# Second feed-forward of a hybrid retention and attention block: weights prepared three steps ahead, turned features fetched by SyncE and used later

## The chip, the core and the metric

The kernel runs on one core of a Trainium2 chip. The metric is device microseconds of one execution, taken as the median of several runs.

## The reference, cut to what matters

One layer with three parts: a feed-forward, a mixer (retention beside sparse attention) and a second feed-forward, for 512 tokens and 16 meta tokens. The change is in the last part, for 512 tokens with D = 1024 and 2816 hidden features, all in fp32.

```python
def swiglu(u, w_gate, w_up, w_down):
    return (jax.nn.silu(u @ w_gate) * (u @ w_up)) @ w_down
...
        h = h + 0.5 * swiglu(rmsnorm(h, ffn1_norm[l]), ffn1_w_gate[l], ffn1_w_up[l], ffn1_w_down[l])
        h = h + hybrid_mixer(rmsnorm(h, mix_norm[l]), pos, k_top, w_in[l], w_ret_out[l], w_att_out[l], w_mix_out[l])
        h = h + 0.5 * swiglu(rmsnorm(h, ffn2_norm[l]), ffn2_w_gate[l], ffn2_w_up[l], ffn2_w_down[l])
    y = rmsnorm(h, final_norm)
```

## The kernel before

An fp32 product is made of three matmuls. Each factor is split in two: the upper part is a copy that ScalarE rounds (L323: `whi` of a weight, `hh` of the features), and the lower part is what VectorE gets by subtracting that copy (L324: `wlo`, `hl`). The products upper by upper, upper by lower and lower by upper are summed in PSUM.

The hidden features of the second feed-forward are done in six units of 512 columns (unit 4 has 256, the narrow one). Gate and up of a unit are 14 steps of twelve matmuls (class `Rows`, `steps`): seven products, each in two halves, of sums and differences of weight quarters and token quarters, so that seven products do the work of eight. `wsum` adds weight quarters on VectorE; `ws` is the buffer of the first sum, and w11, w12, w21 and w22 are the quarters, loaded by SyncE (SP). The results go to PSUM banks named X, Y, Z and V and from there to three rooms A, B and C in SBUF (`copy` on ScalarE, `add` on VectorE). `silu` runs on ScalarE, `gated` multiplies gate and up on VectorE. A and C then hold the gated features of half the tokens each.

The down-projection needs features on the partitions. `turn` does 32x32 transposes on VectorE into `cross`, writes them to DRAM in four stores (`hts`) and loads them back as `land`; stores and load are issued on GpSimd (POOL). `hidden(half)` splits a landed half into `hh` and `hl`. A down step (`down`, L2432) has 24 matmuls; unit i has four of them, woven into the gate and up steps of unit i+1, after steps 4, 7, 10 and 13 (`woven`). `take` adds four finished banks to the tokens on VectorE.

`steps_through` walks through all steps. It loads four steps ahead (`pre`), does the upper split of a step two steps ahead (`upper`) and its lower split in the middle of the present step (`lower`, then `catch_up`, which runs what stands in the list `late`). After a step's matmuls its entries of `posts_of` run: `put(3, ...)` is what follows step 3. On TensorE, ScalarE and VectorE the instructions stand in the order in which this code is written; on SP and POOL a scheduler orders the DMA issues. The weight parts have three buffers each. The down weights are loaded into two buffers `raw` of two halves each.

Of the kernel before, what the change touches and what calls it, by code (L numbers as in the profile page):

```python
# [11 lines left out]
F32 = mybir.dt.float32  # L12
# [69 lines left out]
def kernel(ctx: ExitStack, tc: tile.TileContext, x, meta, g1, wg1, wu1, wd1, gm,  # L82
# [245 lines left out]
    def steps_through(steps):  # L328


        ws = {}

        def pre(i):
            if i < len(steps):
                steps[i][0]()

        def upper(i):
            if i < len(steps):
                v = steps[i][1]()
                n, c = v.shape[1:]  # L340
                at = (*steps[i], w_at[0])[3]
                if len(steps[i]) > 4:
                    hi, lo = steps[i][4]()
                else:
                    hi, lo = (wpool.tile([P, 1024 + WPAD], F32R, tag=t, name=t, bufs=3)[:, at : at + n * c]
                              .rearrange("p (k c) -> p k c", k=n) for t in ("whi", "wlo"))
                ws[i] = (hi, lo, in_two(v, hi, lo))

        def lower(i):
            if i < len(steps):  # L350
                ws[i][2]()

        for i in range(4):
            pre(i)
        for i in range(2):
            upper(i)
            yield
            lower(i)
# [1558 lines left out]
    with pool("ao") as ao:  # L1917
# [219 lines left out]
        pipe = steps_through(steps)  # L2137
# [68 lines left out]
    class Rows:  # L2206
# [11 lines left out]
        FIRST = [("11", "B11", "X"), ("12", "B21", "Z"), ("12", "B22", "V"), ("11", "T2", "X"),  # L2218
                 ("s", "T1", "Y"), ("21", "T3", "X"), ("22", "T4", "X")]
# [29 lines left out]
        def bank(self, name):  # L2249
            tag = {"X": ("x", "d0")[self.first], "V": "d1"}.get(name, "z")  # L2250
            t = f2["ps"].tile([P, 1024], F32, tag=tag, name=f"psq{name}")
            self.d[name] = t.rearrange("p (t c) -> p t c", t=2)[:, :, : self.n]
# [21 lines left out]
        def turn(self, c, to, land, half):  # L2274

            src = self.room[c]
            n = 2 * self.n
            cross = f2["rooms"].tile([P, 1024], F32, tag=f"r{to}", name="cross")[:, :n].rearrange("p (b c t) -> p b c t", t=2, c=32)
# [6 lines left out]
            t = f2["rooms"].tile([P, 1024], F32, tag=f"r{land}", name="land")[:, :n].rearrange("p (k e) -> p k e", k=self.nf)  # L2285
            self.d["land", half] = t
            nc.gpsimd.dma_start(t, d.rearrange("(k p) a e -> p k (a e)", p=P))
# [15 lines left out]
        def steps(self, posts):  # L2303

            def step(i):
# [21 lines left out]
                return (lambda: None, lambda: self.q[n][:, j : j + 2], run)  # L2327
# [27 lines left out]
    def new_t(n):  # L2355
        t = f2["rooms"].tile([P, 1024], F32, tag="rD" if n == 2 else "rC", name=f"ts{n}") if n < 4 else None
# [19 lines left out]
    def fetch_tokens():  # L2376
# [10 lines left out]
        7: (lambda: u0.wsum(2, 0), lambda: u0.wsum(2, 2), fetch_tokens),  # L2387
# [47 lines left out]
    down_raw = []  # L2435
# [9 lines left out]
    def down(u, c, k0, banks, first=True, last=True, posts=(), taken_by=None, parts=None, b3=wide):  # L2445
# [3 lines left out]
        def pre():  # L2449
            if len(down_raw) % 2 == 0:  # L2450
                d["t"] = wpool.tile([P, 2048], F32, tag="raw", name="raw", bufs=2).rearrange("p (k c) -> p k c", k=4)
                down_raw.append(d["t"])
                d["raw"] = d["t"][:, :2]
            else:
                d["raw"] = down_raw[-1][:, 2:]
                down_raw.append(None)
            rows = slice((u.f0 + k0) * P, (u.f0 + k0 + 2) * P)
            nc.sync.dma_start(d["raw"], wd2[rows, c * S : (c + 1) * S].rearrange("(k p) c -> p k c", p=P))
# [59 lines left out]
    def posts_of(u):  # L2518
# [10 lines left out]
        if u.first:  # L2529
            put(0, lambda: u.wsum(4, 0))  # L2530
            put(1, lambda: u.copy("A", "p1", "X"), lambda: u.wsum(4, 2))
            put(2, lambda: new_t(2))
            put(3, lambda: split_t(2), lambda: u.add("A", "Z"))
            put(4, lambda: new_t(3))
            put(5, lambda: split_t(3), lambda: squares(0), lambda: squares(1))
            put(6, lambda: new_t(4), lambda: squares(2), lambda: squares(3), token_norm)
            put(7, lambda: u.copy("B", "u2", "X"), lambda: split_t(4), gate_of("A", 0))
            put(9, lambda: u.copy("C", "p5", "Y"), lambda: u.add("B", "Y"), lambda: u.add("B", "V"), gate_of("B", 1))
            put(11, lambda: u.add("C", "X"))
            loads = {6: "11", 8: "12", 9: "21", 11: "22"}  # L2540
        else:
            make = h4_tile if prev.nf == 2 else hid_tile
            a, b = (1, 3) if u.nf == 4 else (2, 4)
            put(0, lambda: u.wsum(2, 0))
# [10 lines left out]
            loads = {4: "11", 7: "21", 9: "12", 11: "22"}  # L2555
        put(12, lambda: u.gated("C", u.room["C"], u.room["B"], 1), lambda: u.turn("C", "D", "C", 1))
        put(13, lambda: u.gated("A", u.d["X"], u.room["A"], 0), lambda: late.append(lambda: u.turn("A", "B", "D", 0)))
# [3 lines left out]
        if u.first:  # L2561
            late_sums = [lambda: nxt.wsum(1, 0), lambda: nxt.wsum(1, 2)]
            put(13, lambda: late.extend(late_sums))
        return at

    def sums_of(u):
        return (lambda: u.wsum(1, 0), lambda: u.wsum(1, 2))
# [21 lines left out]
    n_units = len(steps)  # L2589
    u4, u5 = units[4:]  # L2590
    c0, c1 = [], []

    def kept_parts():
        t = places.tile([P, 4, S], F32R, tag="w11", name="kept")
        return t[:, 0:2], t[:, 2:4]
# [84 lines left out]
```

## Time and profile before

| | |
|---|---|
| median of 3 runs | 1566.19 us (1564.06 to 1566.45) |
| profiled execution | 1567.81 us, span 1566.0 us |
| mean granted TensorE clock | 0.981 |
| TensorE busy | 1504.8 us (96% of the span) |
| VectorE busy | 1139.6 us (73%) |
| ScalarE busy | 728.9 us (47%) |
| GpSimd busy | 169.9 us (11%) |

The span is the time from the first to the last instruction of the profiled execution. The second feed-forward is its last quarter: its first matmul is at 1149.5 us, its last at 1558. TensorE counts as busy while a matmul runs, also when it runs at the lower clock, so its share of the whole span tells little about one stretch of the program.

### The profile page before, as it was taken

The numbers are of one execution on the slowest core, as the hardware profiler recorded it, in microseconds if no ns is written. First come the engines' busy times: TensorE is split into PE (matmuls) and PEld (weight loads), VectorE is DVE, ScalarE is ACT, GpSimd is POOL, SyncE is SP. The second block draws the span as 40 slices with busy tenths as digits, with TensorE's granted clock in tenths as the row PEclk, the third lists the DMA queues.
The fourth block names the chain that finished last, engine by engine and source line by source line (L and its number), as shares of the span: only waits on it lengthen the run. The fifth ranks groups of instructions, "written<-read, shape, count | busy, mean of one in ns | idle before, by whom it ended". The sixth has DMA issues, their size and how long they took to land. (4 is left out here: it accounts for less than half of the span.)

```text
span 1566.0 us, 22512 instructions
## 1 busy us (share of the span) xinstructions
PE 1504.8 (96%) x8926; PEld 1328.5 (85%) x8926; DVE 1139.6 (73%) x1732; ACT 728.9 (47%) x1044; POOL 169.9 (11%) x250
## 2 busy tenths in 40 slices
PE   9999999999999999999999999999998798898997
PEld 8999999999888889898988889888876576677776
DVE  5997685776887766879787887774687585656765
ACT  5564362554454444433334476672354333433533
POOL 1000000002101020000000322310112010101110
PEclk9999999999999999999999999999999899999999
DMA  4233233247265171323233355664753242423431
GB/s 164 82 108 108 82 102 115 83 128 262 100 225 181 56 238 57 127 91 106 89 98 108 97 170 152 193 198 136 261 165 99 92 137 81 135 68 94 162 108 68
DMA packets 156698, 200.56 MB, mean 128 GB/s; under 512 B 13744, under 2 KB 111688, under 8 KB 155952
## 3 DMA queue, kind: packets, MB, share of 16 engines
q1 hardware_dynamic: 141232, 156.76, 31.0%
q0 software_dynamic: 11680, 35.51, 7.1%
q10 hardware_dynamic: 3680, 6.84, 1.2%
q8 instruction: 70, 1.15, 0.3%
q14 instruction: 36, 0.29, 0.1%
HBM read 168.91 MB, written 30.16 MB: 127 GB/s over the span
## 5 line engine op out<-in xcount | busy, mean ns | idle before, releaser
L324 DVE TENSOR_TENSOR wlo<-raw,whi 128x1024 fp32r<-128x1024 f32 (+2 forms) x155 | 172.5, 1116 | 49.2 <-ACT whi L323 49.1
L323 ACT ACTIVATE whi<-raw 128x1024 fp32r<-128x1024 f32 (+2 forms) x155 | 146.6, 949 | 104.0 <-PE psd L157 33.4
L324 DVE TENSOR_TENSOR wlo<-w,whi 128x1024 fp32r<-128x1024 f32 (+1 forms) x102 | 117.6, 1156 | 81.5 <-ACT whi L323 81.5
L323 ACT ACTIVATE whi<-w 128x1024 fp32r<-128x1024 f32 (+1 forms) x102 | 101.9, 1005 | 121.3 <-PE psd L2432 47.0
L2432 PE MATMUL psd<-whi,hh 128*128 128x512 f32 (+1 forms) x172 | 70.8, 412 | 15.9 <-ACT hh L323 12.2
L2432 PE MATMUL psd<-whi,hl 128*128 128x512 f32 (+1 forms) x172 | 70.8, 412 | 11.9 <-DVE hl L324 11.9
L157 PE MATMUL psro<-vo,whi 128*128 128x512 f32 x256 | 78.8, 389 | 0.0
L2432 PE MATMUL psd<-wlo,hh 128*128 128x512 f32 (+1 forms) x172 | 70.4, 409 | 1.7 <-DVE wlo L324 1.7
L157 PE MATMUL psd<-hl,whi 128*128 128x264 f32 x352 | 71.4, 284 | 0.0
L157 PE MATMUL psd<-hh,wlo 128*128 128x264 f32 x352 | 70.8, 283 | 0.0
L118 DVE TENSOR_TENSOR wlo<-raw,whi 128x1024 fp32r<-128x1024 f32 (+1 forms) x44 | 53.7, 1221 | 23.3 <-ACT whi L117 23.1
L157 PE MATMUL psd<-hh,whi 128*128 128x264 f32 x352 | 70.6, 282 | 0.0
L117 ACT ACTIVATE whi<-raw 128x1024 fp32r<-128x1024 f32 (+1 forms) x44 | 45.4, 1037 | 52.6 <-PE psat L157 17.3
L2319 PE MATMUL psqX<-whi,th 128*128 128x512 f32 (+1 forms) x144 | 56.0, 389 | 9.6 <-DVE p L2263 5.3
L2283 POOL DMA_DIRECT2D hts<-cross x48 | 30.7, 645 | 282.8 <-DVE cross L2280 282.7
L157 PE MATMUL psqX<-tl,whi 128*128 128x264 f32 x216 | 61.2, 283 | 0.0
L157 PE MATMUL psqX<-th,whi 128*128 128x264 f32 x216 | 61.1, 283 | 0.0
L157 PE MATMUL psqX<-th,wlo 128*128 128x264 f32 x216 | 61.1, 283 | 0.0
L2319 PE MATMUL psqX<-wlo,th 128*128 128x512 f32 (+1 forms) x144 | 55.7, 386 | 1.8 <-DVE wlo L324 1.8
L157 PEld LDWEIGHTS psro<-vo,whi 128*128 128x128 f32 x256 | 48.0, 188 | 10.1
L2432 PEld LDWEIGHTS psd<-whi,hh 128*128 128x128 f32 x172 | 35.1, 204 | 24.7 <-ACT hh L323 13.7
L2319 PE MATMUL psqX<-whi,tl 128*128 128x512 f32 (+1 forms) x144 | 55.1, 383 | 0.0
(547 smaller groups left out, 4704.1 us busy)
## 6 DMA issues: line engine op xcount, KB each, us to landing
raw<-in_w_in_dram SPq DMA_DIRECT2D x18, 1024.0 KB, 5.1
raw<-in_w_in_dram SPq DMA_DIRECT2D x33, 512.0 KB, 3.6
raw<-in_ffn_w_down_dram SPq DMA_DIRECT2D x24, 512.0 KB, 4.5
w<-in_w_in_dram SPq DMA_DIRECT2D x24, 512.0 KB, 6.2
raw<-in_ffn_w_up_dram SPq DMA_DIRECT2D x11, 1024.0 KB, 5.0
raw<-in_ffn_w_gate_dram SPq DMA_DIRECT2D x10, 1024.0 KB, 5.0
w<-in_ffn_w_up_dram SPq DMA_DIRECT2D x20, 512.0 KB, 4.7
w<-in_ffn_w_gate_dram SPq DMA_DIRECT2D x20, 512.0 KB, 4.5
```

The costliest lines, as they stand in the source:

```text
L117: nc.scalar.activation(hi, src, AF.Copy)
L118: eng.tensor_tensor(lo, src, hi.bitcast(F32), ALU.subtract)
L157: nc.tensor.matmul(o, a[:, k, :], b[:, sl], start=first and k == 0 and i == 0, stop=last and k == nk - 1 and i == 2, skip_group_check=onto)
L323: nc.scalar.activation(hi, src, AF.Copy)
L324: return lambda: nc.vector.tensor_tensor(lo, src, hi.bitcast(F32), ALU.subtract)
L2283: nc.gpsimd.dma_start(d.rearrange("(b i) a e -> a i b e", i=32)[a], cross[32 * a : 32 * a + 32].rearrange("p b c t -> p b (c t)"))
L2319: nc.tensor.matmul(ps[:, t], a, b[:, k, :], start=not onto and j + k + m == 0, stop=j + k == 3 and m == 2, skip_group_check=onto)
L2432: nc.tensor.matmul(ps, a, m[:, j, cs], start=first and i == 0, stop=last and i == 2)
```

## The change

Six edits, all in the second feed-forward.

1. From the first step of unit 0 to the last such step in the units, the upper split is done three steps ahead (`lead`). Three buffers don't do for that, so every fourth step puts its parts into a fourth pair, `wpair`, which lies in one of the two raw buffers. The down loads then have the two halves of the other one; a second raw buffer is used again by the last two down steps in the units (`last_raw`).
2. The `land` load is issued by SP (`fetch`), not by POOL.
3. The split of the turned features follows steps 2 and 4 in place of 1 and 3 (in the narrow unit 4 and 6 in place of 2 and 4), and the down steps follow steps 7, 9, 11 and 13 (in the narrow unit 8 and 13 in place of 6 and 13).
4. That split goes through its elements in another order: along the tokens, so that it writes next to the last element and reads every second one. Before it went along the pairs, reading next to the last and writing 128 elements further.
5. The first half of the second weight sum (`wsum(2, 0)`) is done with the sums ahead of the unit, not after step 0.
6. The first unit's products come in another order (`FIRST`): the product that used bank V now adds onto Y, which takes out one add on VectorE. The posts of that unit (weight sums, squares, token sums, copies) are placed anew, and the third and fourth token sums use the room of B, not of C. The quarters are loaded after other steps.

```diff
-    def steps_through(steps):
+    def steps_through(steps, lead=lambda i: 2):
...
-            upper(i + 2)
-            steps[i][2](ws.pop(i)[:2], lambda: lower(i + 2))
+            while at["upper"] <= min(i + lead(i), len(steps) - 1):
+                upper(at["upper"])
+                at["upper"] += 1
+            steps[i][2](ws.pop(i)[:2], lowers)
...
+        lead_from, lead_to = KD, []
+        pipe = steps_through(steps, lambda i: 3 if i >= lead_from and (not lead_to or i < lead_to[0]) else 2)
...
-        FIRST = [("11", "B11", "X"), ("12", "B21", "Z"), ("12", "B22", "V"), ("11", "T2", "X"),
-                 ("s", "T1", "Y"), ("21", "T3", "X"), ("22", "T4", "X")]
+        FIRST = [("11", "B11", "X"), ("12", "B21", "Z"), ("s", "T1", "Y"), ("11", "T2", "X"),
+                 ("12", "B22", "Y"), ("21", "T3", "X"), ("22", "T4", "X")]
...
+        def fetch(self, land, half):
+            d = hts[self.i % 2, half, : self.n]
+            t = f2["rooms"].tile([P, 1024], F32, tag=f"r{land}", name="land")[:, : 2 * self.n].rearrange("p (k e) -> p k e", k=self.nf)
             self.d["land", half] = t
-            nc.gpsimd.dma_start(t, d.rearrange("(k p) a e -> p k (a e)", p=P))
+            nc.sync.dma_start(t, d.rearrange("(k p) a e -> p k (a e)", p=P))
...
-                                                         ("p k (q t) -> p k q t", "p k (t q) -> p k q t", "p k (t q) -> p k q t"))]
+                                                         ("p k (q t) -> p k t q", "p k (t q) -> p k t q", "p k (t q) -> p k t q"))]
...
-            if len(down_raw) % 2 == 0:
-                d["t"] = wpool.tile([P, 2048], F32, tag="raw", name="raw", bufs=2).rearrange("p (k c) -> p k c", k=4)
...
+            held = last_raw if (u.i, c, k0) in ((4, 1, 0), (5, 0, 0)) else down_raw
+            if not held:
+                t = wpool.tile([P, 2048], F32, tag="raw", name="raw", bufs=2).rearrange("p (h k c) -> p h k c", h=2, k=2)
+                held.extend(t[:, i] for i in range(2))
+            held.append(held.pop(0))
+            d["raw"] = held[-1]
...
-            put(9, lambda: u.copy("C", "p5", "Y"), lambda: u.add("B", "Y"), lambda: u.add("B", "V"), gate_of("B", 1))
+            put(9, lambda: u.add("B", "Y"), gate_of("B", 1))
...
-            a, b = (1, 3) if u.nf == 4 else (2, 4)
-            put(0, lambda: u.wsum(2, 0))
+            a, b = (2, 4) if u.nf == 4 else (4, 6)
...
-            loads = {4: "11", 7: "21", 9: "12", 11: "22"}
+            loads = {6: "21", 7: "11", 9: "12", 11: "22"}
...
-        return (lambda: u.wsum(1, 0), lambda: u.wsum(1, 2))
+        return (lambda: u.wsum(1, 0), lambda: u.wsum(1, 2), lambda: u.wsum(2, 0))
...
-        woven(i, dict(zip((4, 7, 10, 13), d)))
+        woven(i, dict(zip((7, 9, 11, 13), d)))
...
-    woven(4, {6: d[0], 13: d[1]})
+    woven(4, {8: d[0], 13: d[1]})
...
+    for i in range(lead_from + 3, n_units - 2, 4):
+        steps[i] = (*steps[i], other_parts)
+        lead_to[:] = [i]
```

The first place is VectorE at the start of the third unit, behind the take of the second (a name ends in the number of its tile; `raw` is a down weight, `p1` the room of A). Before:

```order
L324 TENSOR_TENSOR wlo_12552<-w12_12358,whi_12551 128x1024
L2239 TENSOR_TENSOR w11_12186<-ws_12512,w11_12186 128x1024
L324 TENSOR_TENSOR wlo_12574<-w11_12186,whi_12573 128x1024
L324 TENSOR_TENSOR hl_12568<-land_12455,hh_12567 128x4x128x2
L324 TENSOR_TENSOR wlo_12592<-raw_12549,whi_12591 128x1024
L2263 TENSOR_TENSOR p1_12570<-psqZ_12576,p1_12570 128x1024
L324 TENSOR_TENSOR wlo_12612<-w11_12186,whi_12611 128x1024
L324 TENSOR_TENSOR hl_12568<-land_12498,hh_12567 128x4x128x2
```

In the changed kernel, from the same take on:

```order
L324 TENSOR_TENSOR wlo_12534<-w11_12237,whi_12533 128x1024
L2242 TENSOR_TENSOR w11_12237<-ws_12498,w11_12237 128x1024
L324 TENSOR_TENSOR wlo_12553<-w11_12237,whi_12552 128x1024
L324 TENSOR_TENSOR wlo_12573<-ws_12498,whi_12572 128x1024
L324 TENSOR_TENSOR hl_12570<-land_12441,hh_12569 128x4x256
L2266 TENSOR_TENSOR p1_12549<-psqZ_12555,p1_12549 128x1024
L324 TENSOR_TENSOR wpair_11771<-ws_12498,wpair_11771 128x1024
L2242 TENSOR_TENSOR w21_12214<-w22_12385,w11_12237 128x1024
L324 TENSOR_TENSOR wlo_12610<-raw_12158,whi_12609 128x1024
L324 TENSOR_TENSOR hl_12570<-land_12484,hh_12569 128x4x256
```

The sum of the other half of w11 and one split of w12 have moved ahead of the take; a third weight split stands ahead of the first `hl`, and the split into `wpair` and a sum of w21 stand between the two. Counted from the gating of C in front of that take to the second `hl`, there were seven splits of weights, four sums and one add, and there are eight, five and one. The shape of `hl` tells the order of its elements: pairs last before, a half's 256 in one run now.

The second place is the queue of POOL at the same handover, before: stores of C and A and the loads of both.

```order
L2283 DMA hts_11403<-cross_12448 32x16x64 x4
L2283 DMA hts_11403<-cross_12491 32x16x64
L2287 DMA land_12455<-hts_11403 128x4x256
L2283 DMA hts_11403<-cross_12491 32x16x64 x3
L2287 DMA land_12498<-hts_11403 128x4x256
```

In the changed kernel POOL has the eight stores alone, and the loads stand in SP's queue among those of weights.

```order
L2462 DMA raw_12158<-in_ffn2_w_down_dram 128x2x512 x2
L2234 DMA w22_12385<-in_ffn2_w_up_dram 128x2x512 x2
L2462 DMA raw_12158<-in_ffn2_w_down_dram 128x2x512
L2292 DMA land_12441<-hts_11403 128x4x256
L2292 DMA land_12484<-hts_11403 128x4x256
L2462 DMA raw_12158<-in_ffn2_w_down_dram 128x2x512
L2234 DMA w21_12647<-in_ffn2_w_up_dram 128x2x512 x2
L2234 DMA w11_12670<-in_ffn2_w_gate_dram 128x2x512 x2
```

Both lands stand behind a load of a down weight and of w22, and ahead of the next down weight and of w21.

The third place is ScalarE in the first unit, from one of the squares to the splits behind the silu of B. Before (`RR` is a scratch tile, `u2`, `p5` and `p1` are the rooms of B, C and A, `th` the upper part of a token sum):

```order
L2370 ACTIVATE RR_80<-hTok3_11391 128x1024
L323 ACTIVATE whi_11928<-ws_11544 128x1024
L2260 ACTIVATE u2_11944<-psqX_11793 128x1024
L323 ACTIVATE th_11791<-ts2_11844 128x1024
L2268 ACT_TABLE_LOAD
L2268 ACTIVATE p1_11824<-p1_11824,RR_80 128x512 x2
L323 ACTIVATE whi_11949<-w21_11455 128x1024
L323 ACTIVATE whi_11970<-w21_11455 128x1024
L2260 ACTIVATE p5_11986<-psqY_11952 128x1024
L2268 ACTIVATE u2_11944<-u2_11944,RR_80 128x512 x2
L323 ACTIVATE whi_11995<-w22_11497 128x1024
L323 ACTIVATE whi_12011<-w22_11497 128x1024
```

In the changed kernel:

```order
L2375 ACTIVATE RR_80<-hTok2_11390 128x1024
L323 ACTIVATE whi_11927<-w21_11455 128x1024
L2263 ACTIVATE u2_11944<-psqX_11793 128x1024
L323 ACTIVATE th_11791<-ts2_11845 128x1024
L2375 ACTIVATE RR_80<-hTok3_11391 128x1024
L323 ACTIVATE wpair_11771<-w21_11455 128x1024
L2271 ACT_TABLE_LOAD
L2271 ACTIVATE p1_11825<-p1_11825,RR_80 128x512 x2
L323 ACTIVATE whi_11973<-w22_11497 128x1024
L2271 ACTIVATE u2_11944<-u2_11944,RR_80 128x512 x2
L323 ACTIVATE whi_11992<-w22_11497 128x1024
L323 ACTIVATE whi_12011<-w11_11904 128x1024
```

The copy of C (`p5`) has moved ahead of the rows shown, the squares of the last tokens (`hTok3`) have moved behind the copy of B, and the last split is that of the next unit's first quarter.

## Rows read from the trace of the kernel before

**Rows 1.** Chain that ended last: start us, us, engine, line; matmuls of two steps.
```profile
1309.06 2.72 PE psqX L2319 x12
...
1450.24 2.88 PE psqX L2319 x24
```
**Rows 2.** Windows: us, busy (x) of PE, PEld, DVE, ACT, POOL, PEclk, DMA share, GB/s.
```profile
1149.50:1206.00 56.50, 47.06 (x184) 37.17 (x183) 42.51 (x44) 31.12 (x38) 11.40 (x17) 0.91 0.43 140
1206.00:1237.00 31.00, 21.90 (x73) 16.17 (x72) 16.98 (x14) 10.34 (x11) 4.14 (x6) 0.78 0.18 51
1237.00:1278.00 41.00, 41.00 (x182) 33.97 (x181) 27.64 (x40) 15.94 (x17) 2.59 (x4) 1.00 0.49 165
1278.00:1309.00 31.00, 22.89 (x83) 17.64 (x82) 21.65 (x32) 11.48 (x11) 4.12 (x6) 0.83 0.19 53
1350.00:1381.00 31.00, 21.98 (x84) 16.48 (x83) 21.09 (x20) 11.85 (x11) 4.12 (x6) 0.83 0.19 57
1424.00:1449.00 25.00, 18.53 (x96) 15.41 (x95) 14.76 (x19) 9.56 (x13) 3.47 (x5) 0.86 0.20 60
1511.00:1541.00 30.00, 23.71 (x98) 18.79 (x98) 17.03 (x19) 7.44 (x6) 6.74 (x10) 0.94 0.49 158
```
**Rows 3.** Waits of PE from 1149 us on: total us, count, longest.
```profile
PE psd L2432 <- ACT hh L323: 12.2, 4, 4.9
PE psd L2432 <- DVE hl L324: 11.9, 5, 3.3
```
**Rows 4.** Timeline of DVE at the third unit's start: start us, us of the group.
```profile
1271.37 1.41 DVE L2272 SCALAR_TENSOR_TENSOR p<-p,RR,u 128x512 f32<-128x512 f32 x2
...
1282.06 3.71 DVE L2418 SCALAR_TENSOR_TENSOR hTok<-psd,hTok 128x128 f32<-128x128 f32 x16
1285.69 1.22 DVE L2239 TENSOR_TENSOR w<-ws,w 128x1024 f32<-128x1024 f32 x1
1286.82 1.22 DVE L324 TENSOR_TENSOR wlo<-w,whi 128x1024 fp32r<-128x1024 f32 x1
...
1293.26 1.20 DVE L2263 TENSOR_TENSOR p<-psqZ,p 128x1024 f32<-128x1024 f32 x1
1298.58 1.23 DVE L324 TENSOR_TENSOR wlo<-w,whi 128x1024 fp32r<-128x1024 f32 x1 [4.12 <-ACT whi L323]
```
**Rows 5.** Groups by line and form from 1149 us on: busy us, mean ns, idle before.
```profile
L324 DVE TENSOR_TENSOR wlo<-w,whi 128x1024 fp32r<-128x1024 f32 x59 | 71.7, 1219 | 59.1 <-ACT whi L323 59.1
...
L323 ACT ACTIVATE whi<-w 128x1024 fp32r<-128x1024 f32 x59 | 61.7, 1055 | 82.2 <-PE psd L2432 33.2 <-PE psqX L2319 21.6 <-issue 10.6
...
L324 DVE TENSOR_TENSOR hl<-land,hh 128x1024 fp32r<-128x1024 f32 x10 | 20.7, 2067 | 0.6 <-ACT hh L323 0.6
L323 ACT ACTIVATE hh<-land 128x1024 fp32r<-128x1024 f32 x10 | 20.3, 2026 | 25.2 <-DMA land<-hts 25.2
...
L2280 DVE STREAM_TRANSPOSE cross<-p 128x512 f32<-128x512 f32 x20 | 13.0, 688 | 0.0
```
**Rows 6.** Timeline of PE: first matmul behind the last step of unit 1.
```profile
1271.89 0.39 PE L2432 MATMUL psd<-whi,hh 128*128 128x512 f32 x1
```
**Rows 7.** Timeline of POOL at the same handover.
```profile
1279.07 0.65 POOL L2283 DMA_DIRECT2D hts<-cross  x1 [2.19 <-DVE cross L2280]
1279.70 0.77 POOL L2287 DMA_DIRECT2D land<-hts  x1
1280.46 1.95 POOL L2283 DMA_DIRECT2D hts<-cross  x3
1286.00 0.77 POOL L2287 DMA_DIRECT2D land<-hts  x1 [3.59 <-DMA hts<-cross]
```
**Rows 8.** Timeline of ACT and of PE in the first unit.
```profile
1170.48 1.05 ACT L2370 ACTIVATE RR<-hTok 128x1024 f32<-128x1024 f32 x1
...
1194.30 0.77 PE L2319 MATMUL psqX<-whi,th 128*128 128x512 f32 x1 [5.28 <-DVE p L2263]
```
**Rows 9.** Timeline of PE at the last handover.
```profile
1533.86 0.50 PE L2432 MATMUL psd<-whi,hh 128*128 128x512 f32 x1 [1.19 <-ACT hh L323]
...
1535.96 0.50 PE L2432 MATMUL psd<-whi,hl 128*128 128x512 f32 x1 [1.37 <-DVE hl L324]
```

More of the change, by code (lines that the diff above doesn't have):

```diff
@@ L326 @@
     BUSY = {mybir.EngineType.PE, mybir.EngineType.Activation, mybir.EngineType.DVE}
-    def steps_through(steps):
-        ws = {}
+    def steps_through(steps, lead=lambda i: 2):
+        ws, at = {}, {"upper": 2, "lower": 2}
         def pre(i):
@@ L337, in upper, with lowers @@
         def upper(i):
[L338 to L351, printed above, removed]
+            v = steps[i][1]()
+            n, c = v.shape[1:]
+            at_ = (*steps[i], w_at[0])[3]
+            if len(steps[i]) > 4:
+                hi, lo = steps[i][4](n, c)
+            else:
+                hi, lo = (wpool.tile([P, 1024 + WPAD], F32R, tag=t, name=t, bufs=3)[:, at_ : at_ + n * c]
+                          .rearrange("p (k c) -> p k c", k=n) for t in ("whi", "wlo"))
+            ws[i] = (hi, lo, in_two(v, hi, lo))
+        def lowers():
+            while at["lower"] < at["upper"]:
+                ws[at["lower"]][2]()
+                at["lower"] += 1
         for i in range(4):
@@ L357, in steps_through @@
             yield
-            lower(i)
+            ws[i][2]()
             yield
@@ L2249, in bank @@
         def bank(self, name):
-            tag = {"X": ("x", "d0")[self.first], "V": "d1"}.get(name, "z")
+            tag = {"X": ("x", "d0")[self.first], "Y": ("z", "d1")[self.first]}.get(name, "z")
             t = f2["ps"].tile([P, 1024], F32, tag=tag, name=f"psq{name}")
@@ L2272, in gated, with turn @@
                 STT(self.room[c][:, i], up[:, i], rcol[:, 2 * half + i : 2 * half + i + 1], gate[:, i], ALU.mult, ALU.mult)
-        def turn(self, c, to, land, half):
+        def turn(self, c, to, half):
             src = self.room[c]
-            n = 2 * self.n
-            cross = f2["rooms"].tile([P, 1024], F32, tag=f"r{to}", name="cross")[:, :n].rearrange("p (b c t) -> p b c t", t=2, c=32)
+            cross = f2["rooms"].tile([P, 1024], F32, tag=f"r{to}", name="cross")[:, : 2 * self.n].rearrange("p (b c t) -> p b c t", t=2, c=32)
             for t in range(2):
@@ L2355, in new_t @@
     def new_t(n):
-        t = f2["rooms"].tile([P, 1024], F32, tag="rD" if n == 2 else "rC", name=f"ts{n}") if n < 4 else None
+        t = f2["rooms"].tile([P, 1024], F32, tag="rD" if n == 2 else "rB", name=f"ts{n}") if n < 4 else None
         if n < 4:
@@ L2554, in posts_of, with turn_rest @@
             put(11, lambda: u.add("B", "Y"), gate_of("B", 1))
-            loads = {4: "11", 7: "21", 9: "12", 11: "22"}
-        put(12, lambda: u.gated("C", u.room["C"], u.room["B"], 1), lambda: u.turn("C", "D", "C", 1))
-        put(13, lambda: u.gated("A", u.d["X"], u.room["A"], 0), lambda: late.append(lambda: u.turn("A", "B", "D", 0)))
+            loads = {6: "21", 7: "11", 9: "12", 11: "22"}
+        put(12, lambda: u.gated("C", u.room["C"], u.room["B"], 1), lambda: u.turn("C", "D", 1), lambda: u.fetch("C", 1))
+        put(13, lambda: u.gated("A", u.d["X"], u.room["A"], 0), lambda: late.append(turn_rest))
+        def turn_rest():
+            u.turn("A", "B", 0)
+            u.fetch("D", 0)
         if nxt:
@@ L2584, with other_parts, kept_parts @@
         d = four(units[i - 1], ((), (), (), sums_of(units[i + 1])))
-        woven(i, dict(zip((4, 7, 10, 13), d)))
+        woven(i, dict(zip((7, 9, 11, 13), d)))
     d = four(units[3], ((), sums_of(units[5]), (), ()))
-    woven(4, {6: d[0], 13: d[1]})
+    woven(4, {8: d[0], 13: d[1]})
     woven(5, {6: d[2], 13: d[3]})
     n_units = len(steps)
+    pair = []
+    def other_parts(n, c):
+        if not pair:
+            t = wpool.tile([P, 2048], F32R, tag="raw", name="wpair", bufs=2)
+            pair.extend((t[:, :1024], t[:, 1024:]))
+        return [t[:, : n * c].rearrange("p (k c) -> p k c", k=n) for t in pair]
+    for i in range(lead_from + 3, n_units - 2, 4):
+        steps[i] = (*steps[i], other_parts)
+        lead_to[:] = [i]
     u4, u5 = units[4:]
     c0, c1 = [], []
-    def kept_parts():
+    def kept_parts(n, c):
         t = places.tile([P, 4, S], F32R, tag="w11", name="kept")
```

31 lines of the change are left out of this document (12 added, 19 removed).

## The prediction

> **What bounds the kernel now.** I read the stretches of the second feed-forward first, since TensorE's own work in them is known: twelve wide matmuls, one step, take 2.72 us, so one takes 0.2267, and twelve narrow ones (unit 4) take 1.44 [rows 1]. A stretch's length less its matmuls at that price is what TensorE loses in it. In 1237 to 1278 that is nothing (182 matmuls need 41.3 of 41.0 us), at a granted clock of 1.00. The loss sits where one unit hands over to the next, and in the first unit [rows 2]: 14.8 us in the first unit (184 matmuls, 41.7 of 56.5 us); 14.45 before the second (73 matmuls), 12.2 before the third (83), 12.0 before the fourth (84), 10.9 before the narrow one (24 wide and 72 narrow of the 96: 14.1 of 25.0) and 7.8 at the last handover (98). That is 72 us. The reader should see the granted clock beside it: 0.78 to 0.94 there. So the loss is part waiting and part work that follows a wait at the lower of TensorE's two clock levels (1.2, not 2.4 GHz).
>
> Next the waits of TensorE: the two costliest sit on the down-projection, 12.2 us for hh from ScalarE in four waits and 11.9 for hl from VectorE in five [rows 3]. Both are the split of the turned features. Last, VectorE at the third unit's start [rows 4]: from 1271.37 it works without a gap to 1294.4, waits 4.12 us for ScalarE's whi, and does the second hl behind it, which starts 1.15 us after 1298.58 and takes 2.07 [rows 5]: 1301.8. TensorE had finished the last step of the unit before at 1271.89 [rows 6] and had then one down step (24 matmuls, 5.44), five steps (13.6) and two matmuls (0.45) before it needed that hl: 1291.4. It was 10.4 us late; the other 1.8 of the 12.2 are matmuls at the lower clock behind it.
>
> **The change, part by part.** *Later use and lead of three.* Down steps now follow steps 7, 9, 11 and 13, so eight steps lie in front of the first one: 5.44 + 21.76 + 0.45 reaches 1299.5, 8.2 us more cover. VectorE's list up to the second hl, by the order of the changed kernel, is: two gatings (2 x 1.41) and four transposes (4 x 0.69), 5.6; the take, 3.6 (1282.06 to 1285.69); eight wlo, five sums, one add and two hl, sixteen operations that follow each other at 1.13 (1285.69 to 1286.82) [rows 4, 5], 18.1. Sum 27.3. Before it was 5.6 + 3.6 + twelve such operations (13.6) + two hl at some 1.9 (2.07 less what overlaps) = 26.6; lead three and the moved sum add two operations (2.3), the shorter hl give back 1.6. If the gap of 4.1 for whi stays, VectorE ends at 1271.4 + 31.4 = 1302.8, 3.2 us late; without the gap it is in time. I take 3 us of loss in place of 12.2 and 12.0 for the third and fourth units: **-9 each**. For the second unit there is no down step in front and no take: cover 22.2 from the end of the last step, list 27.3 - 3.6 - 0.5 = 23.2, or 27.3 with the gap, late by 1.0 to 5.1; I take 2.5 in place of 14.45: **-12**. In the narrow unit cover grows from seven to nine narrow steps, 2.9 us, and the two hl are 1.7 shorter; with 1 us of clock that comes back, **-5.5** of 10.9. At the tail the waits of 1.19 for hh and 1.37 for hl [rows 9] are the last handover's share, with some slow matmuls behind: **-3.5** of 7.8.
>
> *Split order.* hh takes 2.03 us and hl 2.07, while whi and wlo of the same 128x1024 take 1.06 and 1.22 [rows 5]. The old views go along the pairs, so each next element was written far from the last one; the new one writes next to the last and reads every second element. No row has this form; the nearest is the transpose that writes every second element, 0.69 us for 512, or 1.38 for 1024, against 1.22 for a plain operation. So hl costs between 1.22 and 2.07; by the nearest row I take the low end, and give the high end to a rival. The Trainium skill (SBUF — State Buffer, section "Door 1: The DMA port swizzle (why `[64,N]` ≈ `[32,N]`)") says that the memory works in lines of 16 bytes, that two accesses in a row to a line keep the full rate, and that each access to a new line pays, which the old order does and the new one doesn't. By it the new order costs the plain 1.22; by the transpose row it costs 0.16 more for each hl, 1.5 us over all the handovers, which is inside my range.
>
> *The land loads on SP.* Before, POOL issued one store of A, then the land of C, and three more stores at 1280.46; land A followed at 1286.00, when the stores were down [rows 7]. Four stores in one go save the 0.77 us of that land and nothing more. The transfers themselves are not what ends last: land A was issued at 1286.00, and its hl stood 13 us later. On SP the two lands stand behind one down load and ahead of the next one and of the two loads of w21: SP waits there from the moment it gets to land C until the stores of A have landed, at least the 6.3 us between the two land issues. What is queued behind is used 15 us later or more (the down load after step 11, the w21 sums in the next unit), so I cost it at nothing.
>
> *Buffers.* Every fourth step writes its parts into one of the two raw buffers, so the down loads keep one buffer of two halves. A down load may then be issued only when the one two before it has been split, at worst one step and one down step later (2.72 + 5.44). It costs nothing, by the same slack of 15 us.
>
> *First unit.* ScalarE's string of work from the first square at 1170.48 [rows 8] holds as many instructions as before, but one of VectorE's adds goes, and the split of unit 1's first step (1.13) is now ahead of the last add, on which TensorE waits 5.28 us at 1194.30 [rows 8]. The last square (1.05) now stands behind the copy of B and ahead of the silu, and that copy needs the room that the third token sum used. I choose 0.7 for the square, part of which fills a wait, 1.13 for the split and 0.6, half an operation, for the room: **+2.4**. The edge below is 0 (the add that goes pays for the split), above +5 (as long a wait again as the 5.28).
>
> Sum: -12 - 9 - 9 - 5.5 - 3.5 + 2.4 = -36.6. On the profiled execution (1567.81, span 1566.0) that is 1531.2. The median of the runs lies 1.6 below it, so 1529.6 for the median.
>
> **Rivals.** *Half-rate split.* If reading every second element costs as much as the old order, each handover gets 1.7 us more on VectorE and up to 1.9 more on ScalarE back, over four handovers and the tail 8 to 15 us: 1537 to 1545, about 1541. For it speaks that no row shows the form, against it the transpose.
> *VectorE becomes the bound.* One more wlo and one more sum stand in front of the second hl, and each wlo waits for a whi that ScalarE writes only when a buffer comes free. If the gap doubles (4.1 more) at four handovers, 16.5 us come back: 1546. For it speaks that whi was the one thing that VectorE waited for; against it that a buffer more and a shorter hh loosen ScalarE.
> *SP blocks (slower).* If SP stands at the lands long enough, the raw and weight loads behind them come late, and TensorE waits for weights instead. This begins when the block passes some 15 us, and passes the old time when it adds another 7 us (36.6 over five handovers): a block of 22 us, against 6.3 seen. Then 1575.
> *It doesn't show.* Something else that I did not see, such as the transfers, ends the waits at the same time: 1565.
>
> **How the numbers follow.** Chances: forecast 0.62 (own range 1517 to 1537, from both ends of the gap, the first unit's +5 and a gain of all the slow matmuls), half-rate 0.16, VectorE 0.11, no change 0.04, slower 0.07. A range from 1513 to 1547 leaves out the last two and the far edges of the others. About 0.2% (3 us) is what a measurement of this kernel can tell from no change. Faster 0.89, same 0.04, slower 0.07.
>
> **What would show it.** hh near 1.06 and hl near 1.22 us; the waits for hh and hl down from 12.2 and 11.9 to a few us together; the granted clock of the handover stretches near 1.00; four stores in a row on POOL and lands on SP; the last wait of the first unit near 8 us instead of 5.28. I would be wrong if hh stays at 2, if the wait for wlo on TensorE grows where hl's went, or if DMA loads of raw or w appear among what TensorE's chain ends on.

## The result

The changed kernel takes 1521.57 us in the median (1520.21 to 1523.23, four runs) against 1565.87 for the kernel before (1564.06 to 1566.45, four runs): a ratio of 0.9719, 95% interval 0.9703 to 0.9736. That is 44.3 us less; forecast were 36.6 us less. The profiled execution took 1520.21 us with a span of 1518.4, and the mean granted clock rose from 0.981 to 0.993.

The waits of TensorE from 1145 us on, in the changed kernel (total us, count, longest; they answer to [rows 3]):

```profile
PE psqX L2324 <- DVE p L2266: 8.1, 1, 8.1
PE psd L2437 <- DVE hTok L2430: 3.7, 1, 3.7
PE psd L2437 <- DVE hl L324: 3.4, 4, 1.8
PE psqX L2324 <- ACT u L2263: 2.7, 1, 2.7
PE psqY L2324 <- DVE p L2266: 1.2, 1, 1.2
PE psd L2437 <- DVE wlo L324: 0.6, 1, 0.6
```

The wait for hh is gone from the list, and the one for hl fell from 11.9 to 3.4 us. What is left is led by two waits that the handovers have no part in: 8.1 us in the first unit and 3.7 at the tail. The waits for weights (whi and wlo) fell too, from 17.7 us in all to 1.8. In the kernel before, the largest of them were:

```profile
PE psqZ L2319 <- DVE wlo L324: 6.2, 4, 2.3
...
PE psqX L2319 <- ACT whi L323: 4.3, 3, 2.4
...
PE psqY L2319 <- ACT whi L323: 3.2, 2, 2.5
```

The groups of the split, by form (us busy, mean ns, idle before; compare [rows 5]):

```profile
L324 DVE TENSOR_TENSOR hl<-land,hh 128x1024 fp32r<-128x1024 f32 x10 | 12.2, 1219 | 0.0
...
L323 ACT ACTIVATE hh<-land 128x1024 fp32r<-128x1024 f32 x10 | 11.4, 1140 | 15.7 <-DMA land<-hts 15.7
```

hh went from 2026 to 1140 ns and hl from 2067 to 1219, the same as the plain wlo. By the rule of the Trainium skill (SBUF — State Buffer, section "Door 1: The DMA port swizzle (why `[64,N]` ≈ `[32,N]`)") that two accesses in a row to a line keep the full rate, hl was to cost what the plain wlo does, 1.22, where the transposes' row gave 1.38; for VectorE the trace agrees with the page. ScalarE is not quite at its plain 1.06.

The stretches, cut for the changed kernel (columns as in [rows 2]): the first unit, the handovers before the second, third and fourth unit, the first down step of the narrow unit, and 30 us from the last handover on.

```profile
1148.50:1207.80 59.30, 47.22 (x194) 37.10 (x193) 44.73 (x47) 31.50 (x38) 11.61 (x19) 0.91 0.44 142
1207.80:1237.60 29.80, 28.14 (x122) 22.31 (x121) 22.88 (x20) 16.20 (x17) 1.49 (x3) 1.00 0.34 110
1281.10:1298.50 17.40, 16.98 (x74) 13.44 (x73) 13.80 (x12) 11.09 (x12) 0.00 (x0) 1.00 0.37 129
1342.00:1360.00 18.00, 18.00 (x82) 14.88 (x81) 15.21 (x14) 10.87 (x11) 0.00 (x0) 1.00 0.41 128
1398.70:1407.30 8.60, 6.06 (x25) 4.56 (x25) 5.39 (x8) 2.44 (x5) 0.00 (x0) 1.00 0.62 193
1464.20:1494.20 30.00, 25.45 (x103) 20.28 (x102) 15.28 (x19) 6.33 (x7) 5.15 (x8) 0.89 0.45 140
```

Length less matmuls at 0.2267 us gives what TensorE loses there:

| stretch | before [rows 2] | forecast | measured |
|---|---|---|---|
| first unit | 14.8 | 17.2 | 15.3 (194 matmuls in 59.3) |
| before the second | 14.45 | 2.5 | 2.1 (122 in 29.8) |
| before the third | 12.2 | 3 | 0.6 (74 in 17.4) |
| before the fourth | 12.0 | 3 | 0 (82 in 18.0) |
| before the narrow one | 10.9 | 5.4 | 2.9 (25 in 8.6; none in its steps ahead) |
| last handover | 7.8 | 4.3 | 6.6 (103 in 30.0) |

That is 72.1 us before and 27.5 now, 44.6 less, and the result is 44.3. By the busy time of TensorE in the same windows, 27.2 of the 44.6 are idle time (48.4 before, 21.2 now) and 17.4 are what slow matmuls take above that price (23.7 and 6.3). The granted clock is 1.00 at all four handovers in between, where it was 0.78 to 0.86; in the first unit it is 0.91 as before, and at the tail 0.89 (0.94 before).

VectorE at the third unit's start in the changed kernel (start us, us of the group; compare [rows 4]):

```profile
1256.48 1.41 DVE L2275 SCALAR_TENSOR_TENSOR p<-p,RR,u 128x512 f32<-128x512 f32 x2
...
1275.47 1.23 DVE L324 TENSOR_TENSOR wlo<-w,whi 128x1024 fp32r<-128x1024 f32 x1 [1.19 <-ACT whi L323]
1277.46 1.23 DVE L324 TENSOR_TENSOR wlo<-ws,whi 128x1024 fp32r<-128x1024 f32 x1 [0.77 <-ACT whi L323]
...
1283.31 1.23 DVE L324 TENSOR_TENSOR wpair<-ws,wpair 128x1024 fp32r<-128x1024 f32 x1 [2.35 <-ACT wpair L323]
...
1286.72 1.22 DVE L324 TENSOR_TENSOR hl<-land,hh 128x1024 fp32r<-128x1024 f32 x1
```

And the first matmul of TensorE behind the last step of that unit, and the one that waits for the second hl:

```profile
1259.44 0.62 PE L2437 MATMUL psd<-wpair,hh 128*128 128x512 f32 x2
...
1288.00 0.50 PE L2437 MATMUL psd<-whi,hl 128*128 128x512 f32 x1 [0.39 <-DVE hl L324]
```

The list from the gating of C to the end of the second hl runs from 1256.48 to 1287.94, 31.5 us; forecast were 31.4. The gaps for whi are 1.19, 0.77 and 2.35, together 4.3, forecast 4.1. What differs is where it begins: 3.0 us ahead of the end of the unit's last step (1259.44), not 0.5 ahead as before [rows 4, 6]. So TensorE waits 0.39 us for that hl, not the 3.2 of the forecast.

### The profile page after: what moved, and what is told of

It reads as the page before. It is cut to its first block, busy times and chain, and to the rows that moved or that the text cites. A ratio compares the mean times of both kernels' runs of the same rounds, so it can differ in the third digit from the quotient of the medians.

```text
span 1518.4 us, 22527 instructions
## 1 busy us (share of the span) xinstructions
PE 1486.8 (98%) x8926; PEld 1318.0 (87%) x8926; DVE 1130.1 (74%) x1731; ACT 720.3 (47%) x1044; POOL 160.3 (11%) x238
## 5 line engine op out<-in xcount | busy, mean ns | idle before, releaser
L324 DVE TENSOR_TENSOR wlo<-raw,whi 128x1024 fp32r<-128x1024 f32 (+2 forms) x150 | 166.7, 1114 | 38.6 <-ACT whi L323 38.5
L323 ACT ACTIVATE whi<-w 128x1024 fp32r<-128x1024 f32 (+1 forms) x85 | 85.2, 1007 | 107.8 <-DVE w L2242 32.8
L324 DVE TENSOR_TENSOR wlo<-w,whi 128x1024 fp32r<-128x1024 f32 (+1 forms) x85 | 98.0, 1157 | 47.2 <-ACT whi L323 47.1
L117 ACT ACTIVATE whi<-raw 128x1024 fp32r<-128x1024 f32 (+1 forms) x44 | 45.4, 1036 | 53.2 <-PE psga L157 14.8
L2437 PE MATMUL psd<-whi,hh 128*128 128x512 f32 (+1 forms) x132 | 51.8, 392 | 3.8 <-DVE hTok L2430 3.7
L2437 PE MATMUL psd<-whi,hl 128*128 128x512 f32 (+1 forms) x132 | 51.9, 394 | 3.4 <-DVE hl L324 3.4
L157 PEld LDWEIGHTS psd<-hh,wlo 128*128 128x128 f32 x352 | 54.4, 188 | 0.0
L2324 PE MATMUL psqX<-whi,th 128*128 128x512 f32 (+1 forms) x116 | 43.7, 377 | 10.8 <-DVE p L2266 8.1
L157 PEld LDWEIGHTS psd<-hh,whi 128*128 128x128 f32 x352 | 54.1, 188 | 0.0
L157 PEld LDWEIGHTS psd<-hl,whi 128*128 128x128 f32 x352 | 54.0, 188 | 0.0
L323 ACT ACTIVATE whi<-wsum 128x1024 fp32r<-128x1024 f32 x36 | 38.1, 1059 | 30.5 <-PE psd L157 15.0
```

What stands on the lines that cost most here:

```text
L117: nc.scalar.activation(hi, src, AF.Copy)
L157: nc.tensor.matmul(o, a[:, k, :], b[:, sl], start=first and k == 0 and i == 0, stop=last and k == nk - 1 and i == 2, skip_group_check=onto)
L323: nc.scalar.activation(hi, src, AF.Copy)
L324: return lambda: nc.vector.tensor_tensor(lo, src, hi.bitcast(F32), ALU.subtract)
L2324: nc.tensor.matmul(ps[:, t], a, b[:, k, :], start=not onto and j + k + m == 0, stop=j + k == 3 and m == 2, skip_group_check=onto)
L2437: nc.tensor.matmul(ps, a, m[:, j, cs], start=first and i == 0, stop=last and i == 2)
```

## The experiments

The theory was that VectorE's list stands against TensorE's cover at each handover, so that the later use, the shorter split and the third step of lead each carry some of the gain. The rivals were that the split order alone did it, or that the fetch on SP did.

**Old split order.** All else as changed.

```diff
-("p k (q t) -> p k t q", "p k (t q) -> p k t q", "p k (t q) -> p k t q")
+("p k (q t) -> p k q t", "p k (t q) -> p k q t", "p k (t q) -> p k q t")
```

> The changed kernel with the old order of the split of the turned features (along the pairs), all else kept. Theory (VectorE's list against TensorE's cover): hh and hl go back to 2.0 us each, the list up to the second hl grows by 1.7 us and ScalarE's by 1.9, so the waits for hl grow from 0.4 to 2 to 4 us at each of five handovers: 8 to 15 us slower, 1530 to 1537. Rival (the slow split alone held TensorE): most of the gain goes, 1550 or more. Rival (the earlier fetch is the gain): no change, 1521.

Measured: 1541.80 us, ratio 0.9829 (0.9809 to 0.985). The ratios differ by 0.011, some 17 us of 1566, which is above the 8 to 15 that the theory gave. These are its waits of TensorE:

```profile
PE psd L2437 <- DVE hl L324: 8.8, 5, 2.7
...
PE psqY L2324 <- DVE p L2266: 5.2, 4, 2.9
...
PE psd L2437 <- ACT hh L323: 2.0, 2, 1.2
```

And its windows around the first down step of the third unit and of the narrow one (columns as in [rows 2]):

```profile
1286.00:1302.00 16.00, 13.81 (x50) 10.41 (x51) 12.70 (x11) 10.03 (x11) 0.00 (x0) 0.89 0.19 57
1410.00:1425.00 15.00, 10.61 (x43) 8.21 (x42) 9.09 (x10) 5.59 (x8) 0.00 (x0) 0.77 0.63 213
```

The longer list shows not only in hl (3.4 to 8.8 us) but also in the next operation on VectorE, the add of A, on which a step of the unit waits (1.2 to 5.2). And behind these waits the clock is granted at 0.89 and 0.77 again, where it was 1.00. The 50 matmuls of the first window need 11.3 of 16 us: 4.7 lost, for waits of 2.9 us there (1.38 for the add, 1.48 for hl); with the new order 0.6 are lost at this handover. The part that the expectation left out is that the matmuls behind such waits run slow.

**Lead two.** All else as changed, the fourth pair of buffers too.

```diff
-        pipe = steps_through(steps, lambda i: 3 if i >= lead_from and (not lead_to or i < lead_to[0]) else 2)
+        pipe = steps_through(steps, lambda i: 2 if i >= lead_from and (not lead_to or i < lead_to[0]) else 2)
```

> The changed kernel with the upper split two steps ahead throughout; the fourth pair of buffers stays. Theory (list against cover): the waits for hl stay small, and TensorE waits for whi and wlo of weights again at the handovers, where the kernel before lost some 15 us with such waits and the slow matmuls behind them: 8 to 15 us slower, 1530 to 1537. Rival (the order of the split or the fetch is the whole gain): within 2 us of 1521.

Measured: 1517.80 us, ratio 0.9674 (0.9654 to 0.9694). The theory falls here: the third step of lead is no part of the gain. On the same chip as the changed kernel, in five rounds:

> The changed kernel with lead two again, now beside the changed kernel. Theory (the third step of lead brings nothing at the handovers and puts one more split ahead of the first unit's last add): 2 to 5 us under the changed kernel, from the wait of 8.1 us in the first unit, which was 4.4 with lead two. Rival (the earlier difference was the chip's): within 1.5 us of the changed kernel.

> The changed kernel as it is, beside the three others of this call on one chip. 2.8% under before, as at first.

Measured: lead two 1518.63 us (1517.15 to 1519.71), ratio 0.9679 (0.9664 to 0.9694); the changed kernel 1521.60 (1521.53 to 1522.33), ratio 0.97 (0.9686 to 0.9714). The runs of the two don't overlap and the medians are 3.0 us apart, though the two intervals do touch. The waits of TensorE in the one with lead two:

```profile
PE psqX L2324 <- DVE p L2266: 3.8, 1, 3.8
...
PE psqX L2324 <- ACT whi L323: 2.6, 1, 2.6
PE psd L2437 <- DVE hl L324: 1.8, 2, 1.2
PE psqY L2324 <- DVE wlo L324: 1.4, 3, 0.5
PE psqX L2324 <- DVE wlo L324: 1.2, 2, 0.7
```

The add of the first unit is waited for 3.8 us; in the changed kernel beside it that was 7.5. The waits for weights that the theory wanted back are the lines with whi and wlo, none above 2.6 us in all, and the largest of them is in the first unit too. Most of the 3.0 us lie there: the first unit loses 12.5 us with lead two (195 matmuls in 56.7) and 14.9 in the changed kernel beside it (196 in 59.3). Counted from the unit's first matmul, the add comes 2.4 us later in the changed kernel (44.94 against 42.50 us). Ahead of it VectorE has one more split there, which takes its turn of 1.14 us, and one more wait for whi, 1.21 us.

**The land load on POOL.**

```diff
-            nc.sync.dma_start(t, d.rearrange("(k p) a e -> p k (a e)", p=P))
+            nc.gpsimd.dma_start(t, d.rearrange("(k p) a e -> p k (a e)", p=P))
```

> The changed kernel with the land load issued by POOL again. Theory (list against cover): land A comes some 3 us later, and its hl stands 13 us or more behind it in VectorE's list, so within 2 us of 1521. Rival (the fetch on SP is the gain): waits for hh come back, 15 us or more slower, 1537 and above.

Measured: 1523.75 us, ratio 0.9713 (0.9689 to 0.9736), the same as the changed kernel's 0.9719 and 0.97. One wait for hh comes back, of 1.5 us; in the time the queue on which the load is issued makes no difference that can be seen. In the changed kernel the two lands of the third unit's handover lie in one group of SP's timeline, 6.55 us from the first's start to the second's end, so 6.2 us from issue to issue; on POOL they were issued at 1265.46 and 1272.09, 6.6 us apart.

```profile
1264.17 6.55 SPq L2292 DMA_DIRECT2D land<-hts  x2
```

**Early use.** The old places of the split and the down steps, all else as changed.

```diff
-            a, b = (2, 4) if u.nf == 4 else (4, 6)
+            a, b = (1, 3) if u.nf == 4 else (2, 4)
...
-        woven(i, dict(zip((7, 9, 11, 13), d)))
+        woven(i, dict(zip((4, 7, 10, 13), d)))
...
-    woven(4, {8: d[0], 13: d[1]})
+    woven(4, {6: d[0], 13: d[1]})
```

> The changed kernel with the turned features split and used at the old places (split after steps 1 and 3, down steps after 4, 7, 10 and 13; in the narrow unit after 2 and 4, and 6 and 13). Theory (list against cover): 8.2 us of cover go at three handovers and 2.9 at the narrow one, and the clock falls behind the waits: 25 to 35 us slower, 1547 to 1557, nearly all in waits for hh and hl. Rivals (the split order or the fetch is the gain): at most 5 us slower, 1527 or less.

Measured: 1562.17 us, ratio 0.9956 (0.9941 to 0.997): nearly all of the gain goes, 37 us by the ratios. That is a little above the 25 to 35 us expected. These are the waits of TensorE in this kernel:

```profile
PE psd L2437 <- ACT hh L323: 21.7, 4, 6.4
PE psd L2437 <- DVE hl L324: 9.5, 5, 2.6
```

And SP's issues at the third unit's start:

```profile
1275.86 0.37 SPq L2292 DMA_DIRECT2D land<-hts  x1
1287.13 0.37 SPq L2462 DMA_DIRECT2D raw<-in_ffn_w_down_dram  x1
1287.66 0.37 SPq L2292 DMA_DIRECT2D land<-hts  x1
```

The scheduler has put a down load between the two lands. It goes out at 1287.13, when VectorE has split a down weight (1285.89 and 1.22 us), and land A, whose four stores were issued from 1275.86 on, follows at 1287.66, 11.8 us after land C. This is the slower rival's mechanism the other way round: there the lands were to hold up the weights, here a weight holds up a land. How much that costs is read from ScalarE, at the third unit and at the narrow one:

```profile
1290.54 1.33 ACT L2271 ACTIVATE p<-p,RR 128x512 f32<-128x512 f32 x2 [3.40 <-DVE p L2266]
1292.36 1.12 ACT L323 ACTIVATE hh<-land 128x1024 fp32r<-128x1024 f32 x1 [0.48 <-DMA land<-hts]
...
1435.06 1.12 ACT L323 ACTIVATE hh<-land 128x1024 fp32r<-128x1024 f32 x1 [6.42 <-DMA land<-hts]
```

At the third unit ScalarE does the hh of A behind the silu of A, which waits for VectorE's add, and then it waits only 0.48 us for the land (0.43 and 0.42 at the second and fourth unit). There VectorE's list holds the hh up, not the load. At the narrow unit, where land A is issued at 1430.47, 13.9 us after land C, the load does: 6.42 us. In the changed kernel the lands stand next to each other, and the later use gives slack besides. So this run doesn't give the price of the later use by itself; the next ones do, from the kernel before.

**Later use alone, split order alone, and both,** each as an edit of the kernel before.

```diff
-            a, b = (1, 3) if u.nf == 4 else (2, 4)
+            a, b = (2, 4) if u.nf == 4 else (4, 6)
...
-        woven(i, dict(zip((4, 7, 10, 13), d)))
+        woven(i, dict(zip((7, 9, 11, 13), d)))
...
-    woven(4, {6: d[0], 13: d[1]})
+    woven(4, {8: d[0], 13: d[1]})
```

> The kernel before with one edit: the turned features are split and used at the later places. Theory (later use and the short split together are the gain, each worth less alone): the old list of 30.7 us with 2 us for each hl against the longer cover leaves a few us of waits at each handover, as with the old split order in the changed kernel: 25 to 32 us faster than before. Rival (the later use needs the third step of lead): at most 15 us faster.

> The kernel before with one edit: the new order of the split of the turned features. Theory: hh and hl fall to 1.1 and 1.2 us, but the down steps still come too early, so the waits for hh and hl shrink by some 2 us at each of five handovers: 5 to 12 us faster than before. Rival (the split order holds TensorE by itself): 25 us or more faster.

> The kernel before with two edits: later use and new split order; lead two, three buffers, the land load on POOL and the old first unit stay. Theory: these two are the whole gain, 42 to 50 us faster than before, waits for hh and hl under 5 us in all. Rival (lead three, the fourth buffer, the fetch on SP or the new first unit carry part of it): 30 us or less, with waits for weights at the handovers.

Measured on one chip, against 1567.72 us before: the later use alone 1536.36, ratio 0.9799 (0.9774 to 0.9823); the split order alone 1553.73, 0.9911 (0.9888 to 0.9933); both 1522.18, 0.9708 (0.9686 to 0.9729). In per cent that is 2.0, 0.9 and 2.9: the two add up, and together they are as much as the whole change, without the lead, the buffer, the fetch and the first unit. That doesn't make all of these worth nothing: the changed kernel with lead two stands at 0.9674 and 0.9679, some 5 us under the two edits alone, so the others may bring a little that the third step of lead takes away. The intervals overlap, and none of the others but the fetch was tried by itself. The later use alone was worth 31 us and both 45.5, as expected; the split order alone was worth 14, above the 5 to 12 expected. The waits for the split with the later use alone:

```profile
PE psd L2432 <- DVE hl L324: 2.9, 2, 1.5
...
PE psd L2432 <- ACT hh L323: 0.5, 1, 0.5
```

With the split order alone:

```profile
PE psd L2432 <- ACT hh L323: 8.5, 4, 3.2
PE psd L2432 <- DVE hl L324: 8.4, 5, 2.6
```

With both:

```profile
PE psd L2432 <- ACT hh L323: 1.3, 1, 1.3
...
PE psd L2432 <- DVE hl L324: 1.2, 2, 0.6
```

With the later use alone hh is hardly waited for though it takes 2.08 us, as in the kernel before, and the waits for hl are 2.9 us. With the split order alone both waits are still at 8.5 and 8.4, for the down steps come as early as before. With both they are 2.5 us together.

The traces also show why VectorE's list begins earlier with the later use. The gating of C stands behind VectorE's add of B, which needs the products of step 11. In the kernel before only two steps lie between step 11 and the end of the unit, and the add waits for step 11's bank; it starts 5.2 us ahead of that end. With the later use the third down step stands behind step 11 and not behind step 10, and the add starts 9.2 us ahead (1250.29 against 1259.44), without a wait. The place of that down step was not tried by itself. The add of B, before and in the changed kernel:

```profile
1266.65 1.23 DVE L2263 TENSOR_TENSOR u<-psqY,u 128x1024 f32<-128x1024 f32 x1 [0.40 <-PE psqY L2319]
...
1250.29 1.22 DVE L2266 TENSOR_TENSOR u<-psqY,u 128x1024 f32<-128x1024 f32 x1
```

**The first unit.** The rest of the loss is there, so three runs took on the wait for the add of C. This is VectorE there in the changed kernel:

```profile
1191.27 2.36 DVE L324 TENSOR_TENSOR wlo<-w,whi 128x1024 fp32r<-128x1024 f32 x2 [2.35 <-ACT whi L323]
1193.55 1.22 DVE L2266 TENSOR_TENSOR p<-psqX,p 128x1024 f32<-128x1024 f32 x1
```

And TensorE:

```profile
1194.91 0.77 PE L2324 MATMUL psqX<-whi,th 128*128 128x512 f32 x1 [8.10 <-DVE p L2266]
```

TensorE waits 8.1 us for that add; VectorE does it behind two weight splits, for whose whi it waited 2.35 us, and ScalarE writes them behind the silu of B.

```diff
-            put(8, gate_of("A", 0))
-            put(9, lambda: u.add("B", "Y"), gate_of("B", 1))
-            put(11, lambda: u.add("C", "X"))
+            put(9, lambda: u.add("B", "Y"))
+            put(11, lambda: u.add("C", "X"), gate_of("B", 1), gate_of("A", 0))
```

> The changed kernel with the two silu of the first unit moved from behind steps 8 and 9 to behind the last add of that unit (after step 11). Theory: TensorE's 8.1 us wait for that add is VectorE standing behind two splits whose whi ScalarE writes only after the silu of B; without it the add comes 4 to 6 us earlier, and the time falls by as much (about 2.9 to 3.2% under before). Rival (the add waits for its own bank, or the silu then hold the next unit's whi): within 2 us of the changed kernel.

Measured: 1520.45 us, ratio 0.9698 (0.9672 to 0.9724); the wait fell from 8.1 to 4.3 us. By time alone this can't be told from the changed kernel, so the 4 to 6 us expected are not shown. The profiled execution was the fastest of the four, at 1517.33 us; the others took 1520.29 to 1520.96. Its wait, from the list of TensorE's waits:

```profile
PE psqX L2324 <- DVE p L2266: 4.3, 1, 4.3
```

The same edit together with lead two:

> The changed kernel with lead two and the first unit's two silu behind its last add. Theory: both edits shorten what stands ahead of that add, the wait falls from 8.1 to some 3 us: 5 us under the changed kernel, 1 to 2 under lead two alone. Rival (both shorten the same wait for ScalarE): as lead two alone.

Measured: 1513.61 us (1511.77 to 1513.96), ratio 0.9645 (0.963 to 0.966), 8.0 us under the changed kernel beside it and 5.0 under lead two alone, clear of both and above the 5 and 1 to 2 expected. This is the fastest of all kernels run. Its add on VectorE now waits for TensorE's X itself:

```profile
1189.29 1.23 DVE L2266 TENSOR_TENSOR p<-psqX,p 128x1024 f32<-128x1024 f32 x1 [1.14 <-PE psqX L2324]
```

TensorE waits 1.4 us for it:

```profile
1190.66 0.47 PE L2324 MATMUL psqX<-whi,th 128*128 128x512 f32 x1 [1.41 <-DVE p L2266]
```

And the window of the first unit:

```profile
1149.20:1201.50 52.30, 46.68 (x194) 36.64 (x193) 43.30 (x46) 31.21 (x38) 11.56 (x19) 0.97 0.49 153
```

The first unit loses 8.3 us in this window (194 matmuls in 52.3), 15.3 in the changed kernel.

> The same, and the third and fourth squares, the norm and the add of B stand behind the last add of the first unit too. Theory: ScalarE copies B some 2.5 us earlier (TensorE waits 2.7 us for that copy) and VectorE's last add has one operation less ahead of it: 4 to 6 us under the run with the late silu. Rival (what is moved then holds the next unit's splits or the gating of C): no faster, with new waits at the next unit's start.

```diff
-            put(6, lambda: split_t(3), lambda: squares(1), lambda: new_t(4), lambda: squares(2))
-            put(7, lambda: u.copy("B", "u2", "X"), lambda: split_t(4), lambda: squares(3), token_norm)
-            put(9, lambda: u.add("B", "Y"))
-            put(11, lambda: u.add("C", "X"), gate_of("B", 1), gate_of("A", 0))
+            put(6, lambda: split_t(3), lambda: squares(1), lambda: new_t(4))
+            put(7, lambda: u.copy("B", "u2", "X"), lambda: split_t(4))
+            put(11, lambda: u.add("C", "X"), lambda: u.add("B", "Y"), lambda: squares(2), lambda: squares(3), token_norm, gate_of("B", 1), gate_of("A", 0))
```

Measured: 1515.74 us (1513.60 to 1518.38), ratio 0.9662 (0.9645 to 0.9679): no faster. The rival was right: TensorE now waits 2.4 us for wlo at the next unit's second product, a wait that the run with the late silu doesn't have. From its list of waits:

```profile
PE psqZ L2324 <- DVE wlo L324: 2.9, 2, 2.4
```

## Why the prediction was right

The time, the sign and the place were right: the range of 1513 to 1547 holds 1521.57, and the gain is at the handovers, in the waits for hh and hl, in those for weights ahead of them and in the slow matmuls behind. That VectorE's list, not the transfer, holds the handover shows in the kernel before too: ScalarE waits 3.08 us for the land of C at the third unit, but VectorE has no gap there, and the hh of A stands behind a silu for which ScalarE waits 5.50 us for VectorE's add. By its steps:

- *Cover against list at the third and fourth unit* (-9 each forecast; measured -11.6 and -12): the list of 31.4 us and its gap of 4.1 came out as 31.5 and 4.3. The term that was mis-sized is the start: VectorE was taken to begin as late as before. The gating of C begins 3.0 us ahead of the last step's end now, and 3.2 us of waiting became 0.4. This start comes with the later use: it is 0.5 us ahead in the kernel before and with the split order alone (1266.89 against 1267.41), 2.9 with the later use alone (1259.68 against 1262.62) and with both (1256.87 against 1259.81). What goes with it is the add of B, which starts earlier since the third down step now stands behind step 11. With so short a wait hardly any slow matmuls follow. The gap for whi did not double, so the rival in which VectorE becomes the bound did not come true either.
- *Second unit* (-12; measured -12.4): right.
- *Narrow unit* (-5.5; measured -8): its waits are 1.84 us for hl and 0.60 for wlo, and the clock stayed at 1.00. The term left out is the waits for weights in its steps ahead of the down step, 4.5 us before (2.52 the longest) and none now.
- *Tail* (-3.5; measured -1.2): too large. The wait of 1.19 for hh went and that of 1.37 for hl became 0.81, but the 3.7 us for the take, which no edit touches, stayed, and the clock granted there is 0.89, lower than the 0.94 before.
- *First unit* (+2.4; measured +0.5): the place was right, the wait for the add of C grew from 5.28 to 8.1. All waits of TensorE in the unit together grew from 9.4 to 12.1 us, 2.6 more, which is close to the forecast. In them one shrank that was not thought of (the second product waited 2.35 us for wlo and now waits 0.41), and one of 2.67 for the copy of B stands where one of 1.29 for whi stood. What the sum left out is the slow matmuls: they cost 5.3 us before and 3.2 now, so the stretch as a whole hardly changed.
- *Fetch on SP and the buffers at nothing:* the run with the land on POOL bears it out for the fetch, and SP stood 6.2 us between the lands, near the 6.3 reckoned, while TensorE waits for no weight longer than 0.6 us from the first unit on. The buffers were not tried by themselves; the run with both edits of the kernel before, which has the old buffers, is as fast as the changed kernel.
- *Rival of the half-rate split* (about 1541, 0.16): it did not come true, but the old order put back into the changed kernel took 1541.8.
- *Third step of lead:* the prediction counted its extra operation on the list, and otherwise took it as part of the cover. The runs show that it brings nothing and costs some 3 us, of which 2.4 are in the first unit: one more split and one more wait for whi ahead of the add, for which TensorE waits 3.7 us less with lead two. The prediction had counted 1.13 for that split.

The sum came out 7.7 us too small (8.1 by the stretches): the third and fourth unit gave 5.6 us more than forecast, the narrow one 2.5, the second 0.4 and the first unit 1.9, and the tail 2.3 less. The tail errs against the rest, and it is luck that its error hides part of theirs. Behind the first two of these gains stands also that a handover nearly without a wait keeps the clock: it was granted at 1.00 in all of them. The old-split run shows it from the other side: waits of 2.9 us cost 4.7.

## What to carry to other kernels

Where two engines in written order meet, add up the list of the one from a fixed point and the cover of the other, and take the start of the list from the same stretch, since its lateness may be part of what the change removes. Before adding lead or buffers, look whether the late item is the weight or the thing beside it: here the time at which features were used and the order of their elements brought as much as all six edits, and more lead only put another operation ahead of a waited one. An access order that jumps on the write side can nearly double a plain copy (2.03 us against 1.06 on ScalarE), and takes one line to turn round.

## What the runs showed of the hardware that was not expected

ScalarE's copy and VectorE's subtract of 128x1024 fp32 take 2.03 and 2.07 us in the old order, where the two elements of a pair are written 512 bytes apart, and 1.14 and 1.22 when each is written next to the last and every second element is read. Reading at a step of 8 bytes cost VectorE nothing against its plain 1.22. ScalarE's copy had the jump on the write side alone; VectorE in the old order also read hh with that jump, so for VectorE the runs don't part the two sides. The issue of the same 512 KB land load stands at 0.37 us on SP and 0.77 on POOL.
